# A decoder layer with retrieved experts: the pace of the gathers, a later exponential, wider selection matrices and rows loaded by chunk

## The chip, the cores and the metric

The kernel runs on 1 core of one Trainium2 chip. The metric is the device time in microseconds (us) of one execution. The core has five engines that each run their own instruction list in order: TensorE (PE in the profile; its weight loads are PEld), VectorE (DVE), ScalarE (ACT), GpSimd (POOL) and SyncE (SP), which here only starts DMA transfers. Engines wait for each other by semaphores.

## The reference

One layer works on 256 tokens of 2048 floats. It has an attention part with 16 heads, a retrieval of single-neuron experts (PEER), and a gated embedding, each followed by a layer norm. The change lies in the last two:

```python
    q = (xt @ wq).reshape(t, PEER_HEADS, PEER_QDIM)
    ...
    top, sel = lax.top_k(cand, PEER_TOPK)
    eidx = jnp.take_along_axis(cidx, sel, axis=-1)
    gates = jax.nn.softmax(top, axis=-1)
    ...
        ub = u[eb]
        vbk = v[eb]
        act = jax.nn.gelu(jnp.einsum('thed,td->the', ub, xb).astype(jnp.float32))
        w = (gb * act).astype(xb.dtype)
        return jnp.einsum('the,thed->td', w, vbk)
    ...
        gate = jax.nn.sigmoid(jnp.einsum('bsd,de->bse', x, ple_gate[i]))
        emb = jnp.einsum('bsk,kd->bsd', p[i], ple_proj[i])
        x = layer_norm(alpha * x + gate * emb, ln_g[i, 2], ln_b[i, 2])
```

There are 8 heads with 16 chosen experts each, so 128 experts per token, out of 16384 rows in `u` and `v`.

## The kernel before

The tokens are treated in two ways. For the first 100 tokens (groups of 64, 32 and 4, `GROUPS`) the chosen rows of `peer_u` and `peer_v` are gathered from memory. For the other 156 tokens all 16384 experts are computed densely, and a matrix of gates, zero almost everywhere, picks the chosen ones.

**Dense u stage** (L971 and L982). 128 blocks `u_block`, one for each `ia`: a load `wf` of 1 MB on SP's queue (a ring of 5 tiles), 16 matmuls in one PSUM bank (L208, two records each in the trace), and ScalarE's gelu L950, which empties the bank into `A1` (first 64 blocks) or `A2`. Four banks go round. Beside each of the first 64 blocks one step of `topk_work` runs: top-16 searches on VectorE, the choice among candidates (products L691 on POOL), and `gates(t)`, the softmax of the gates: subtract L707 on VectorE, exponential L711 on ScalarE, sum and division L714 to L716. A `yield` ends a step, so the number of yields says how many blocks lie between two parts of it in program order. Beside the blocks 64 to 127 `gate_work` runs: for 5 tokens at a time, VectorE compares to make one-hot matrices (L897, L899), ScalarE scales them (L903, L904), TensorE multiplies them in pairs into `ps_G` (L911, L912), and VectorE multiplies the result into `A1` (L921).

**Dense v stage** (L1024 and L1034). 128 blocks for the first half of the outputs, then 128 for the second; a block is 8 matmuls (L1000), and two blocks share a load of 1 MB. The first 64 run with `gate_work` for `A2`. The last six blocks are held back (`STAG`) and come after `sparse_out`.

**Gathers.** 200 transfers of 1 MB, 100 of u rows and then 100 of v rows, from `sparse_work`: each is a tiny DMA `mark` on SP's queue (L856), a copy of it on POOL (L857), and the indirect DMA on POOL (L859) into a ring of 4 tiles `gb`. SP's queue holds the marks between the loads, so a mark lands about when the loads ahead of it do, and POOL goes no further before. VectorE uses the gathered tile in L832 (product with the token, summed) or in L842 (weighted sum). `gathers(n)` adds `n` to `due` after every block and starts a gather whenever `due` reaches 1: `GQ` beside the queries, `GU` in the u stage, `GV` in the v stage. `sparse_out` (L869) then sums and transposes the weighted rows with selection matrices `sel`, 64, 32 and 4 columns wide, by matmuls L876.

**Gated embedding.** After layer norm 2 the transposed input `X2` is multiplied with `ple_gate` in four chunks of 512 columns (`gate_mm`), whose weights are split into a high and a low part by ScalarE (L109) and VectorE (L110). `gate_out` loads the embedding `em` on POOL's queue (L1128), takes the sigmoid on ScalarE (L1130), and multiplies and adds on VectorE (L1131, L1132). The `x2` that it adds to must be scaled by rows of layer norm 2 first: `natural_x2` loads `g_row` and `b_row`, copied to all partitions, and POOL does a multiplication and an addition (L578, L579) for each chunk and token half: chunk 0 with rows on POOL's queue, chunks 1 to 3 at once after chunk 0, with rows on SP's queue. `finish` normalizes and stores.

In code wrapped in `keep` an engine's instructions stay in the order in which the program lists them; the rest is placed by a scheduler.

Of the kernel before, what the change touches and what calls it, by code (L numbers as in the profile page):

```python
# [9 lines left out]
F32 = mybir.dt.float32  # L10
# [4 lines left out]
ALU = mybir.AluOpType  # L15
# [4 lines left out]
P = 128  # L20
T = 256
NT = T // P
D = 2048
ND = D // P
NCH = D // 512
# [13 lines left out]
SEG1 = 64  # L39
# [7 lines left out]
SELB = 8  # L47
NGB = 4

GQ = 1.8  # L50
GU = 0.7
GV = 0.35
GSCALE = 2.0 ** 15
GB = 5
OHB = 5
# [102 lines left out]
def build(tc, a, out):  # L158
    nc = tc.nc
# [367 lines left out]
    for c in range(NCH):  # L527
        s = slice(c * 512, (c + 1) * 512)
# [47 lines left out]
    def affine(xt, c, gr, br):  # L576
        s = slice(c * 512, (c + 1) * 512)
        nc.gpsimd.tensor_tensor(xt[:, s], xt[:, s], gr[:, s], op=ALU.mult)  # L578
        nc.gpsimd.tensor_tensor(xt[:, s], xt[:, s], br[:, s], op=ALU.add)  # L579
# [14 lines left out]
    gin = pools.open("gin", "left", bufs=1)  # L594
# [7 lines left out]
    nc.gpsimd.memset(zero, 0.0)  # L602
    sel, eig, eact, ew = [], [], [], []
    for i, (_, n) in enumerate(GROUPS):
        sel.append(gin.tile([P, n], F32, name=f"sel{i}"))
        nc.gpsimd.dma_start(sel[i], a[f"c_sel{i}"])

        eig.append(gin.tile([P, 2, n], U32, name=f"eig{i}"))
        eact.append(gin.tile([P, n], F32, name=f"eact{i}"))
        ew.append(gin.tile([P, n], F32, name=f"ew{i}"))  # L610
# [50 lines left out]
    keep = tc.keep_in_program_order  # L661
# [42 lines left out]
    def gates(t):  # L704

        g = gate[:, t]
        keep(nc.vector.tensor_tensor(g, CV[:, t], CV[:, t, :, 0:1].to_broadcast([P, PH, TOPK]),  # L707
                                     op=ALU.subtract))
        yield
        yield  # L710
        keep(nc.scalar.activation(g, g, AF.Exp))  # L711
        for _ in range(6):
            yield
        keep(nc.vector.tensor_reduce(gs[:, t], g, axis=AX.X, op=ALU.add))  # L714
        nc.vector.reciprocal(gs[:, t], gs[:, t])
        nc.vector.tensor_tensor(g, g, gs[:, t, :, None].to_broadcast([P, PH, TOPK]), op=ALU.mult)  # L716
        if t == 0:
            nc.vector.tensor_copy(eg[:NSP, 1].bitcast(F32), g[:NSP])
            for i in range(len(GROUPS)):
                slots(i, 1, by_slot(i, 1))  # L720
            gated.append(t)
        yield
# [69 lines left out]
    def gathers(n):  # L792

        nonlocal due
        due += n
        while due >= 1:
            due -= 1
            run(sparse, 1)
# [70 lines left out]
    def sparse_out():  # L869

        for i, (t0, n) in enumerate(GROUPS):
            per = min(ND, 512 // n)
            for d0 in range(0, ND, per):
                ps = pbank(pp, "ps_y")
                for j in range(per):
                    keep(nc.tensor.matmul(ps[:, j * n:(j + 1) * n],  # L876
                                          ys[i][:, (d0 + j) * P:(d0 + j + 1) * P], sel[i],
                                          start=True, stop=True))
                nc.scalar.copy(yT[:, d0:d0 + per, t0:t0 + n],
                               ps[:, :per * n].rearrange("p (j t) -> p j t", j=per))  # L880

    def gate_work(oh, parts, s0, ns, group):

# [76 lines left out]
    for hh in range(2 * PH):  # L960
# [3 lines left out]
        if hh > 2:  # L964
            gathers(GQ)
    bg.flush()
# [4 lines left out]
    for ia in range(SEG1):  # L971
        u_block(ia, W_of(ia))
        run(work, 1)
        gathers(GU)
    while not run(work, 1):
# [6 lines left out]
    for ia in range(SEG1, NIA):  # L982
        u_block(ia, W_of(ia))
        run(work, 1 + (ia % 8 == 7))
        gathers(GU)
    while not run(work, 1):
        pass

# [35 lines left out]
    for ia in range(NIA):  # L1024
        if ia >= SEG1:
            while not done:
                done = run(work, 1)
        v_block(0, ia, psv)
        if not done:
            done = run(work, 1 + (ia % 8 == 7))  # L1030
        gathers(GV)
    pools.close("ohp")
    psv2 = v_banks(pa)
    for ia in range(SEG1):  # L1034
        v_block(1, ia, psv2)
        gathers(GV)
    pools.close("a1p")
# [3 lines left out]
    x2 = [l2.tile([P, D], F32, name=f"x2_{t}") for t in range(NT)]  # L1041
# [29 lines left out]
    for ia in range(SEG1, NIA - STAG):  # L1071
        v_block(1, ia, psv2, keep if ia >= NIA - STAG - 16 else lambda ins: ins)
        gathers(GV)
        if ia in (NIA - STAG - 9, NIA - STAG - 5):
# [28 lines left out]
    l3 = pools.open("l3", "left", bufs=1)  # L1103
# [21 lines left out]
    def gate_out(c, t, ps, c0, n):  # L1125
        s = slice(c * 512 + c0, c * 512 + c0 + n)
        em = l3.tile([P, 512], F32, name="em", tag="em", bufs=3)[:, :n]
        keep(nc.gpsimd.dma_start(em, a["s_emb"][t * P:(t + 1) * P, s]))  # L1128
        sig = l3.tile([P, 512], F32, name="sig", tag="sig", bufs=3)[:, :n]
        keep(nc.scalar.activation(sig, ps, AF.Sigmoid))  # L1130
        keep(nc.vector.tensor_tensor(sig, sig, em, op=ALU.mult))  # L1131
        keep(nc.vector.scalar_tensor_tensor(x2[t][:, s], x2[t][:, s], ALPHA, sig,  # L1132
                                            op0=ALU.mult, op1=ALU.add))
        for j in range(c0, c0 + n, 256):
            nc.vector.bn_stats(st3[t][:, 2 * c + j // 256, :],
                               x2[t][:, c * 512 + j:c * 512 + j + 256])
# [18 lines left out]
    ln2(0)  # L1155
    ln2(1, range(ND // 8))

    g_row = l3.tile([P, D], F32, name="g_row", tag="g_row")
    b_row = l3.tile([P, D], F32, name="b_row", tag="b_row")

    def natural_x2(c0, c1, queue):

        s = slice(c0 * 512, c1 * 512)
        for dst, src in ((g_row, "ln_g"), (b_row, "ln_b")):
            keep(queue.dma_start(dst[:, s], a[src][1:2, s].to_broadcast([P, s.stop - s.start])))
        for c in range(c0, c1):
            for t in range(NT):
                affine(x2[t], c, g_row, b_row)


    sg.order = sg2.order = keep
# [3 lines left out]
    for half in range(2):  # L1175
        for t in range(NT):
            gate_mm(pss[t], t, parts[half], 0, 512, half * ND // 2)
        if not half:
            natural_x2(0, 1, nc.gpsimd)
    for c in range(NCH):  # L1180
        if c == NCH - 1:
            gate_out(c, 1, ps_half, 256, 256)
            break
        gate_out(c, 0, pss[0], 0, 512)
        first = gate_parts(c + 1, 0)
        gate_out(c, 1, pss[1], 0, 512)
        parts = first + gate_parts(c + 1, 1)
        if c == 0:
            natural_x2(1, NCH, nc.sync)
        if c == 1:  # L1190
            gr3, br3 = ln_rows(l3, 2)
        if c < NCH - 2:
            pss = [pbank(pa, "ps_gate") for _ in range(NT)]
            for t in range(NT):
                gate_mm(pss[t], t, parts, 0, 512)
            continue
        pss = [pbank(pa, "ps_gate") for _ in range(3)]
        gate_mm(pss[0], 0, parts, 0, 512)
        gate_mm(pss[1][:, :256], 1, parts, 0, 256)
        gate_mm(pss[2][:, :256], 1, parts, 256, 256)  # L1200
        gate_out(c + 1, 0, pss[0], 0, 512)
        gate_out(c + 1, 1, pss[1][:, :256], 0, 256)
        ps_half = pss[2][:, :256]
# [5 lines left out]
def _constants():  # L1209
    pos = np.arange(T, dtype=np.float32)  # L1210
    inv = np.float32(ROPE_THETA) ** (-np.arange(0, ROT, 2, dtype=np.float32) / np.float32(ROT))
    ang = (pos[:, None] * inv[None, :].astype(np.float32)).astype(np.float32)
    cos, sin = np.cos(ang).T, np.sin(ang).T
    h = ROT // 2
    C = np.ones((P, T), np.float32)
    S = np.zeros((P, T), np.float32)
    for s in (0, 64):
        C[s:s + h] = cos
        C[s + h:s + 2 * h] = cos
        S[s:s + h] = -sin  # L1220
# [6 lines left out]
    return {  # L1227
        "c_ropeC": C, "c_ropeS": S, 
        "c_svalid": svalid, "c_sneg": sneg,
        "c_dmask": np.concatenate([np.zeros((P, P), np.float32), dm], axis=1),  # L1230
        "c_tri": (r[:, None] >= r[None, :]).astype(np.float32),
        "c_ones": np.ones((P, P), np.float32),
        "c_ident": np.eye(P, dtype=np.float32),
        **{f"c_sel{i}": (np.arange(P)[:, None] // (P // n) == np.arange(n)[None, :]).astype(np.float32)
           for i, (_, n) in enumerate(GROUPS)},
        "c_iota": np.broadcast_to(np.arange(P, dtype=np.float32), (P, P)).copy(),
    }
# [71 lines left out]
```

## Time and profile before

| what | value |
|---|---|
| time, median of 3 runs | 1824.08 us (1823.42 to 1825.66) |
| the profiled execution | 1825.47 us |
| its span, first to last instruction | 1823.7 us |
| mean granted clock of TensorE | 0.988 |
| TensorE, matmuls | 1772.4 us busy |
| VectorE | 1058.7 us busy |
| ScalarE | 540.0 us busy |
| GpSimd | 548.6 us busy |
| DMA, the whole span | 609.04 MB, mean 334 GB/s |

Lines such as L950 are lines of the kernel. A window of the trace gives, for each engine, the busy time in that stretch with the number of instructions, then TensorE's granted clock (1.00 is full speed), the busy share of the DMA engines, and GB/s. In a wait, `PE ps_u L208 <- DMA wf<-peer_u` reads: TensorE at L208 waited for the transfer into `wf`. A timeline joins instructions of one kind into a row with its count; the bracket says how long the engine was idle before and what released it. A matmul of the u blocks, the v blocks and `sparse_out` leaves two records, and a row's count is that of records. A wait for several semaphores is put down to the one that came last.

### The profile page before, as it was taken

The page shows a single profiled execution, that of the slowest core. Times are in us where ns is not written, and L with a number is a line of the kernel's source. Part 1 is how long each engine was busy: PE and PEld are TensorE (multiplying, and loading weights), DVE is VectorE, ACT ScalarE, POOL GpSimd, SP SyncE. Part 2 cuts the span into 40 slices and gives each one's busy share as a digit, 9 for nine tenths or more (in the row PEclk, how much of TensorE's full clock was granted, in tenths as well). Part 3 has the DMA queues.
Part 4 walks back from the last instruction along what each step waited for, and adds up shares of the span by engine and source line. Part 5 has one row for each costly group of instructions (what it writes and reads, how often), then busy time and mean ns, then how long its engine had stood idle before and what let it go on. Part 6 is the DMA issues. An engine that isn't in the chain of part 4 may idle for free.

```text
span 1823.7 us, 30383 instructions
## 1 busy us (share of the span) xinstructions
PE 1772.4 (97%) x12110; PEld 1663.8 (91%) x12110; DVE 1058.7 (58%) x1659; ACT 540.0 (30%) x1351; POOL 548.6 (30%) x581
## 2 busy tenths in 40 slices
PE   8999999999998999999999999999999999999986
PEld 7888888888897999899999999999999999999866
DVE  5555688654588995545555546674343333333786
ACT  5687477642011001004333315550000000001532
POOL 0133133005465244232223222333243222221241
PEclk9999999999999999999999999999999999998999
DMA  7544644657899999999999999999999999997461
GB/s 281 189 167 162 231 147 155 234 204 263 310 376 415 415 420 419 421 420 420 411 401 406 399 404 407 371 379 387 420 420 420 419 418 417 421 420 330 155 256 52
DMA packets 99726, 609.04 MB, mean 334 GB/s; under 512 B 12872, under 2 KB 14720, under 8 KB 35424
## 3 DMA queue, kind: packets, MB, share of 16 engines
q1 hardware_dynamic: 66784, 384.24, 53.5%
q0 software_dynamic: 31072, 218.28, 29.7%
q10 hardware_dynamic: 1728, 4.59, 0.6%
q8 instruction: 95, 1.56, 0.3%
q14 instruction: 47, 0.39, 0.1%
HBM read 600.40 MB, written 6.55 MB: 333 GB/s over the span
## 4 chain that ended last, share of the span: by engine, by line
PE 85%; DMA 9%; DVE 4%; ACT 1%; issue 1%; POOL 0%; SPq 0%; DVEq 0%; ACTq 0%; POOLq 0%
PE ps_v L1000 27%; PE ps_u L208 25%; PE ps_qk L197 7%; PE ps_q L208 6%; DMA wf<-peer_u 4%; DMA wf<-peer_v 4%; PE ps_qk L199 3%; PE ps_v L216 2%; PE ps_v L217 2%; PE ps_mix L215 2%; PE ps_mix L216 2%; PE ps_mix L217 2%; PE ps_v L215 2%; DVE wl L110 1%; DMA gb<-u_rows,eig 1%; PE ps_gate L216 1%
## 5 line engine op out<-in xcount | busy, mean ns | idle before, releaser
L208 PE MATMUL ps_u<-XF,wf 128*128 128x156 f32 x4096 | 559.0, 298 | 15.5 <-ACT A L950 9.3
L208 PEld LDWEIGHTS ps_u<-XF,wf 128*128 128x128 f32 x4096 | 549.0, 191 | 18.4 <-ACT A L950 15.4
L1000 PE MATMUL ps_v<-A,wf 128*128 128x156 f32 x4096 | 555.7, 298 | 4.8 <-DMA wf<-peer_v 4.7
L1000 PEld LDWEIGHTS ps_v<-A,wf 128*128 128x128 f32 x4096 | 547.7, 191 | 7.3 <-DMA wf<-peer_v 6.7
L842 DVE SCALAR_TENSOR_TENSOR y<-gb,ew,y 128x2048 f32<-128x2048 f32 x94 | 221.0, 2351 | 258.0 <-DMA gb<-v_rows,eig 257.9
L832 DVE SCALAR_TENSOR_TENSOR gb<-gb,xq 128x2048 f32<-128x2048 f32 x100 | 229.1, 2295 | 171.5 <-DMA gb<-u_rows,eig 165.8
L110 DVE TENSOR_TENSOR wl<-wf,wh 128x1024 fp32r<-128x1024 f32 (+1 forms) x201 | 222.6, 1132 | 114.9 <-ACT wh L109 113.2
L109 ACT CAST wh<-wf 128x1024 fp32r<-128x1024 f32 (+1 forms) x201 | 173.1, 890 | 359.7 <-DMA wf<-ple_gate 250.3
L857 POOL COPY pace<-mark 1x1 f32<-1x1 f32 x200 | 107.2, 536 | 564.5 <-DMA mark<-c_iota 564.1
L197 PE MATMUL ps_qk<-X,wh 128*128 128x512 f32 x512 | 185.2, 401 | 0.0
L859 POOL DMA_INDIRECT gb<-u_rows,eig x100 | 126.7, 1267 | 145.2 <-DVE gb L832 62.2
L950 ACT ACTIVATE A<-ps_u 128x156 f32<-128x156 f32 x128 | 38.2, 301 | 433.3 <-PE ps_u L208 360.7
L859 POOL DMA_INDIRECT gb<-v_rows,eig x100 | 130.9, 1309 | 54.7 <-issue 32.2
L199 PE MATMUL ps_qk<-X,wl 128*128 128x256 f32 x512 | 145.7, 285 | 0.0
L197 PEld LDWEIGHTS ps_qk<-X,wh 128*128 128x128 f32 x512 | 96.4, 188 | 22.0 <-issue 1.0
L903 ACT ACTIVATE hi<-eq,ghf 128x64 f16<-128x64 f16 x312 | 104.5, 335 | 39.4 <-DVE eq L897 38.1
L208 PE MATMUL ps_q<-XF,wf 128*128 128x256 f32 x512 | 113.5, 379 | 0.0
L208 PEld LDWEIGHTS ps_q<-XF,wf 128*128 128x128 f32 x512 | 95.9, 190 | 12.3
L904 ACT ACTIVATE lo<-eq,glf 128x64 f16<-128x64 f16 x312 | 104.3, 334 | 0.0
L199 PEld LDWEIGHTS ps_qk<-X,wl 128*128 128x128 f32 x512 | 96.3, 188 | 2.5 <-issue 1.3
L1019 ACT COPY XF<-ps_v 128x312 f32<-128x312 f32 x8 | 3.4, 420 | 188.8 <-PE ps_v L1000 188.5
L216 PE MATMUL ps_gate<-wl,X 128*128 128x512 f32 (+1 forms) x144 | 53.9, 376 | 4.8 <-DVE wl L110 4.6
(242 smaller groups left out, 1768.0 us busy)
## 6 DMA issues: line engine op xcount, KB each, us to landing
wf<-peer_u SPq DMA_DIRECT2D x128, 1024.0 KB
wf<-peer_v SPq DMA_DIRECT2D x128, 1024.0 KB
wf<-w_qk SPq DMA_DIRECT2D x64, 512.0 KB
wf<-w_out SPq DMA_DIRECT2D x32, 512.0 KB
wf<-peer_wq SPq DMA_DIRECT2D x16, 1024.0 KB
wf<-ple_gate SPq DMA_DIRECT2D x16, 1024.0 KB
wf<-w_v SPq DMA_DIRECT2D x31, 512.0 KB
mark<-c_iota SPq DMA_DIRECT2D x200, 0.0 KB
```

The lines of the kernel that those rows point to most:

```text
L109: self.order(nc.scalar.copy(wh, src))
L110: self.order(nc.vector.tensor_tensor(wl, src, wh.bitcast(F32), op=ALU.subtract))
L197: nc.tensor.matmul(ps, wh[:, j * P:(j + 1) * P], xt[:, dt, :], start=dt == 0, stop=False)
L199: nc.tensor.matmul(ps[:, :T], wl[:, j * P:(j + 1) * P], xt[:, dt, :T], start=False, stop=dt == ND - 1)
L208: nc.tensor.matmul(ps[:, :T - t0], wf[:, dt * P:(dt + 1) * P], xt[:, dt, t0:], start=dt == 0, stop=dt == ND - 1)
L216: nc.tensor.matmul(ps, hi, wl, start=False, stop=False)
L832: keep(nc.vector.scalar_tensor_tensor(g, g, 1.0, xq[i], op0=ALU.mult, op1=ALU.mult, accum_out=eact[i][:, j:j + 1]))
L842: keep(nc.vector.scalar_tensor_tensor(ys[i], g, ew[i][:, j:j + 1], ys[i], op0=ALU.mult, op1=ALU.add))
L857: keep(nc.gpsimd.tensor_copy(pace, mark))
L859: keep(nc.gpsimd.indirect_dma_start(out=g, out_offset=None, in_=a[kind], in_offset=bass.IndirectOffsetOnAxis(ap=eig[i][:, 0, j:j + 1], axi ...
L903: nc.scalar.mul(hi[:, j, :], eq[:, j, :], ghf[:, t])
L1000: return nc.tensor.matmul(ps[:, (j % 2) * NDT:(j % 2 + 1) * NDT], vf[:, j * P:(j + 1) * P], W_of(ia), start=False, stop=ia == NIA - 1 and ...
```

## The change

Four edits, independent of each other.

- **Pacing of the gathers.** Blocks with one-hot products get a larger rate than those without: in the u stage 0.64 and 0.75 in place of 0.7, in the v stage 0.42 for the first 64 blocks and 0.33 for the rest in place of 0.35. The number of gathers stays.
- **Exponential of the gates.** Between the subtraction and the exponential lie nine yields in place of two.
- **Selection matrices.** They are at least 32 columns wide, so that of the third group grows from 4 to 32 (the added columns are zero), and its products are packed 16 to a bank; the copy takes the first `n` columns of each.
- **Rows for scaling.** `natural_x2` takes one chunk at a time, with its rows in a tile of two times 512 columns (two such tiles in turn). For chunks 1 to 3 it is called after the chunk before, with the rows on SP's queue; third-norm rows now get tiles of their own. The sigmoid's tile goes from three buffers to two.

```diff
-GU = 0.7
-GV = 0.35
+GU, GUG = 0.64, 0.75
+GV, GVG = 0.33, 0.42
...
-        sel.append(gin.tile([P, n], F32, name=f"sel{i}"))
+        sel.append(gin.tile([P, max(n, 32)], F32, name=f"sel{i}"))
...
                                      op=ALU.subtract))
-        yield
-        yield
+        for _ in range(9):
+            yield
         keep(nc.scalar.activation(g, g, AF.Exp))
...
         for i, (t0, n) in enumerate(GROUPS):
-            per = min(ND, 512 // n)
+            m = max(n, 32)
+            per = min(ND, 512 // m)
             for d0 in range(0, ND, per):
                 ps = pbank(pp, "ps_y")
                 for j in range(per):
-                    keep(nc.tensor.matmul(ps[:, j * n:(j + 1) * n],
+                    keep(nc.tensor.matmul(ps[:, j * m:(j + 1) * m],
                                           ys[i][:, (d0 + j) * P:(d0 + j + 1) * P], sel[i],
                                           start=True, stop=True))
                 nc.scalar.copy(yT[:, d0:d0 + per, t0:t0 + n],
-                               ps[:, :per * n].rearrange("p (j t) -> p j t", j=per))
+                               ps[:, :per * m].rearrange("p (j t) -> p j t", j=per)[:, :, :n])
...
     for ia in range(SEG1, NIA):
         u_block(ia, W_of(ia))
         run(work, 1 + (ia % 8 == 7))
-        gathers(GU)
+        gathers(GUG)
...
-        gathers(GV)
+        gathers(GVG if ia < SEG1 else GV)
...
-        sig = l3.tile([P, 512], F32, name="sig", tag="sig", bufs=3)[:, :n]
+        sig = l3.tile([P, 512], F32, name="sig", tag="sig", bufs=2)[:, :n]
...
-    def natural_x2(c0, c1, queue):
-
-        s = slice(c0 * 512, c1 * 512)
-        for dst, src in ((g_row, "ln_g"), (b_row, "ln_b")):
-            keep(queue.dma_start(dst[:, s], a[src][1:2, s].to_broadcast([P, s.stop - s.start])))
-        for c in range(c0, c1):
-            for t in range(NT):
-                affine(x2[t], c, g_row, b_row)
+    def natural_x2(c, queue):
+
+        s = slice(c * 512, (c + 1) * 512)
+        gb = l3.tile([P, 2, 512], F32, name="gb_rows", tag="gb_rows", bufs=2)
+        for i, src in enumerate(("ln_g", "ln_b")):
+            keep(queue.dma_start(gb[:, i], a[src][1:2, s].to_broadcast([P, 512])))
+        for t in range(NT):
+            nc.gpsimd.tensor_tensor(x2[t][:, s], x2[t][:, s], gb[:, 0], op=ALU.mult)
+            nc.gpsimd.tensor_tensor(x2[t][:, s], x2[t][:, s], gb[:, 1], op=ALU.add)
...
         parts = first + gate_parts(c + 1, 1)
-        if c == 0:
-            natural_x2(1, NCH, nc.sync)
+        natural_x2(c + 1, nc.sync)
         if c == 1:
             gr3, br3 = ln_rows(l3, 2)
```

The third group's products stay in one PSUM bank (16 x 32 = 512 columns).

More of the change, by code (lines that the diff above doesn't have):

```diff
@@ L1156, in build @@
     ln2(1, range(ND // 8))
-    g_row = l3.tile([P, D], F32, name="g_row", tag="g_row")
-    b_row = l3.tile([P, D], F32, name="b_row", tag="b_row")
-    def natural_x2(c0, c1, queue):
-        s = slice(c0 * 512, c1 * 512)
-        for dst, src in ((g_row, "ln_g"), (b_row, "ln_b")):
-            keep(queue.dma_start(dst[:, s], a[src][1:2, s].to_broadcast([P, s.stop - s.start])))
-        for c in range(c0, c1):
-            for t in range(NT):
-                affine(x2[t], c, g_row, b_row)
+    def natural_x2(c, queue):
[6 more added lines that the diff above has]
+            nc.gpsimd.tensor_tensor(x2[t][:, s], x2[t][:, s], gb[:, 1], op=ALU.add)
     sg.order = sg2.order = keep
@@ L1178, in build @@
         if not half:
-            natural_x2(0, 1, nc.gpsimd)
+            natural_x2(0, nc.gpsimd)
     for c in range(NCH):
@@ L1233, in _constants @@
         "c_ident": np.eye(P, dtype=np.float32),
-        **{f"c_sel{i}": (np.arange(P)[:, None] // (P // n) == np.arange(n)[None, :]).astype(np.float32)
+        **{f"c_sel{i}": (np.arange(P)[:, None] // (P // n) == np.arange(max(n, 32))[None, :]).astype(np.float32)
            for i, (_, n) in enumerate(GROUPS)},
```

## The prediction

> **What bounds the kernel now.** I read the page's head and its DMA part first, then the waits of TensorE, then windows cut at the edges of the stages, and last the timelines of the places where TensorE stands still.
>
> ```profile
> span 1823.7 us, 30383 instructions
> ...
> PE 1772.4 (97%) x12110; PEld 1663.8 (91%) x12110; DVE 1058.7 (58%) x1659; ACT 540.0 (30%) x1351; POOL 548.6 (30%) x581
> ...
> GB/s 281 189 167 162 231 147 155 234 204 263 310 376 415 415 420 419 421 420 420 411 401 406 399 404 407 371 379 387 420 420 420 419 418 417 421 420 330 155 256 52
> ...
> wf<-peer_u SPq DMA_DIRECT2D x128, 1024.0 KB
> wf<-peer_v SPq DMA_DIRECT2D x128, 1024.0 KB
> ```
>
> TensorE is busy for 97%, so an edit can win only the remaining 51 us and what runs at half clock. The GB/s line shows a second limit: from slice 12 to slice 35 (547 to 1641 us) it lies between 371 and 421 and never above. The transfers there are the expert weights, 1 MB each, and the 200 gathers, also 1 MB each (128 x 2048 floats, by the L842 row quoted below).
>
> ```profile
> PE ps_u L208 <- ACT A L950: 9.3, 2, 8.9
> PE ps_u L208 <- DMA wf<-peer_u: 6.2, 10, 1.9
> ...
> PE ps_v L1000 <- DMA wf<-peer_v: 4.7, 5, 2.2
> PE ps_gate L216 <- DVE wl L110: 4.6, 5, 1.7
> ...
> PE ps_G L911 <- ACT hi L903: 0.6, 1, 0.6
> ```
>
> Waits of TensorE: total, times, longest. One stall is on ScalarE's copy of a u block; ten waits are for u weights, five for v weights, five for the splits of the gate weights, and one of 0.6 us for a one-hot product.
>
> ```profile
> 540.00:660.00 120.00, 111.08 (x818) 110.73 (x817) 109.33 (x314) 10.27 (x30) 47.72 (x62) 0.96 1.01 416
> 660.00:719.00 59.00, 57.96 (x436) 57.55 (x436) 40.33 (x67) 7.29 (x19) 32.70 (x38) 1.00 1.01 419
> 719.00:785.00 66.00, 60.91 (x449) 59.24 (x447) 32.80 (x35) 5.19 (x18) 16.03 (x21) 1.00 1.01 421
> 838.00:1117.00 279.00, 279.00 (x2318) 277.64 (x2317) 149.09 (x179) 89.16 (x364) 79.92 (x90) 1.00 1.00 407
> 1117.00:1255.00 138.00, 138.00 (x1256) 135.97 (x1256) 91.24 (x111) 73.42 (x302) 37.69 (x40) 1.00 0.97 379
> 1255.00:1551.00 296.00, 296.00 (x2236) 296.00 (x2235) 115.50 (x50) 1.68 (x4) 94.34 (x96) 1.00 1.01 417
> 1551.00:1671.00 120.00, 115.15 (x843) 113.21 (x841) 48.01 (x28) 4.36 (x8) 31.18 (x36) 0.99 1.01 421
> ```
>
> Windows: length, busy time of PE, PEld, DVE, ACT, POOL, granted clock, DMA share, GB/s. The first three lie in the first 64 u blocks, the fourth in the other 64 (with one-hot products), the fifth in the v blocks with products, the last two in the v blocks after them. Where TensorE loses time, the DMA stands at 416 to 421; where it loses none, there is room (407 and 379). So the bytes of the stages without products are too many and those of the stages with products too few: 421 is my ceiling.
>
> **Edit 1, pacing.** A u block takes 4.24 us where nothing is late (timelines: start, length, engine, line, operation, and in brackets the idle time before and what ended it):
>
> ```profile
> 730.98 0.30 ACT L950 ACTIVATE A<-ps_u 128x156 f32<-128x156 f32 x1 [3.94 <-PE ps_u L208]
> 735.22 0.30 ACT L950 ACTIVATE A<-ps_u 128x156 f32<-128x156 f32 x1 [3.94 <-PE ps_u L208]
> ...
> 758.36 0.30 ACT L950 ACTIVATE A<-ps_u 128x156 f32<-128x156 f32 x1 [4.67 <-PE ps_u L208]
> 763.34 0.30 ACT L950 ACTIVATE A<-ps_u 128x156 f32<-128x156 f32 x1 [4.67 <-PE ps_u L208]
> ...
> 711.88 0.96 POOL L859 DMA_INDIRECT gb<-u_rows,eig  x1 [3.83 <-DVE gb L832]
> ...
> 716.85 0.96 POOL L859 DMA_INDIRECT gb<-u_rows,eig  x1 [3.83 <-DVE gb L832]
> ...
> 754.35 1.98 POOL L857 COPY pace<-mark 1x1 f32<-1x1 f32 x1 [5.04 <-DMA mark<-c_iota]
> ```
>
> At 758 a block takes 4.98 us, and it is a load that is late. Earlier, at 712, one gather is issued every 4.97 us and waits for its buffer, not for its pacing mark; the first long wait for a mark is at 754. So until about 750 the gathers are behind their program and take half of the DMA, whatever the pace says; a smaller pace only brings the end of this catching up nearer.
>
> Demand of a first-half u block: 1 load and 0.70 gathers of 1.0486 MB in 4.24 us is 420 GB/s, right at the ceiling, so a lost ring is never refilled. At 0.64 it is 406.
>
> Gain: from 534.59 (the first u block) to 754, less the 11.6 us of edit 2, lie about 46 blocks (208 us at some 4.5 each). While both kinds share evenly, a block works off 1 - 0.70 = 0.30 of a backlog, so about 14 gathers were behind; at 0.36 a block that takes 39 blocks. Seven blocks fewer at 0.74 us lost each are 5.2 us, and after them nothing pushes the demand to the ceiling. The bound from above: windows two and three hold 885 block matmuls of 4.24/32 us, 117.3 us of work in 125, so 7.7 us can be won; by bytes, 64 x 0.06 = 3.8 gathers fewer are 9.6 us of DMA at 421. I take 5.5; ends 2 and 7.7.
>
> Last v stage: a load feeds two v blocks (1.06 us for 8 matmuls each, 16 records), so 0.5 of a load and 0.35 gathers per block; at the 417 to 421 measured, 0.33 asks for 0.83/0.85 of it, 407 to 411. The wait is at the end: 843 matmuls of 0.1325 us are 111.7 us of work in 120, 8.3 lost, of which 4.7 is the listed wait. With 0.07 x 64 = 4.5 gathers more done before and 0.02 x 122 = 2.4 fewer issued here, the stage has some 4 MB (9 us of DMA) less to move. Two loads of gate weights (L1076) fall into it still, so not all goes. I take 5.5; ends 2 and 8.3.
>
> Given back: in the second half of u the demand rises to 407 x 1.75/1.70 = 419, under 421 by nothing much; in the v stage with products to 379 x 0.92/0.85 = 410. I take +1 for a few new waits; ends 0 and +10 (64 x 0.05 = 3.2 gathers plus 1 of backlog at 2.5 us).
>
> **Edit 2, the exponential of the gates 7 u blocks later.**
>
> ```profile
> 588.69 0.31 ACT L711 ACTIVATE gate<-gate 128x128 f32<-128x128 f32 x1 [22.17 <-DVE gate L707]
> ...
> 534.59 3.34 PE L208 MATMUL ps_u<-XF,wf 128*128 128x156 f32 x24
> ...
> 590.76 70.83 PE L208 MATMUL ps_u<-XF,wf 128*128 128x156 f32 x512 [8.92 <-ACT A L950]
> 662.08 4.48 PE L208 MATMUL ps_u<-XF,wf 128*128 128x156 f32 x32 [0.49 <-DMA wf<-peer_u]
> 667.11 13.09 PE L208 MATMUL ps_u<-XF,wf 128*128 128x156 f32 x97 [0.55 <-DMA wf<-peer_u]
> ```
>
> ScalarE runs in order: at L711 it stands 22.17 us for VectorE's subtract, which is deep in the top-k work. The block copies L950 queued behind it come late, the four PSUM banks fill, and TensorE stands 8.92 us; then it starts slowly (the window's mean clock is 0.96). Nine yields instead of two put seven blocks' copies, 7 x 4.24 = 30 us, ahead of L711, and 30 is more than 22: the stall goes. The first window prices it: 818 matmuls of 0.1325 us are 108.4 us of work in 120, so 11.6 were lost, 8.92 of it the gap. But 72 us later TensorE waits for a load anyway, and the DMA carried 416 of 421 all through: while TensorE stood, the loads filled the ring. What really comes free is 120 x (421 - 416)/421 = 1.4 us. I take 1; ends 0 and 11.6. The nine yields of the second token half lengthen the top-k work from 46 to 53 steps, one a block, still short of the 64 blocks after which the products need its results. The POOL products of L691 that stood in one clump come apart between gathers, which holds no buffer longer.
>
> **Edit 3, 32 columns for the last group.**
>
> ```profile
> 1670.61 7.23 PE L876 MATMUL ps_y<-sel,y 128*128 128x64 f32 x64
> 1677.67 6.61 PE L876 MATMUL ps_y<-sel,gb 128*128 128x4 f32 x32
> ...
> 1678.20:1688.20 10.00, 10.00 (x45) 9.97 (x46) 0.00 (x0) 0.47 (x2) 0.00 (x0) 0.50 0.01 4
> ```
>
> The 64- and 32-column matmuls start every 0.113 us, the 4-column ones every 0.207, with the clock at 0.50 from 1678.2 on, which costs 5 us in 10. The clock fell although TensorE had no gap; it fell when 64 narrow matmuls had been through, and 32 columns are narrow too. I take -0.5; ends 0 and -5. By the Trainium skill (TensorE: Matmul & The Clock Gate, Part 1: The HAM clock gate) half clock follows a window of some 3.4 us without activity; here no row shows such a gap, so by that rule alone the thin stream must have counted as idle, and 32 columns might count as busy, which would give the 5.
>
> **Edit 4, rows of the scaling chunk by chunk.**
>
> ```profile
> 1736.00:1765.00 29.00, 24.24 (x97) 17.27 (x96) 26.72 (x31) 9.32 (x18) 17.09 (x13) 1.00 0.61 222
> 1765.00:1787.00 22.00, 22.00 (x98) 18.08 (x97) 12.03 (x22) 9.51 (x19) 1.09 (x2) 1.00 0.52 204
> ...
> 1731.00 9.79 POOL L578 TENSOR_TENSOR x<-x,g_row 128x512 f32<-128x512 f32 x6 [12.60 <-DMA g_row<-ln_g]
> 1740.76 10.18 POOL L579 TENSOR_TENSOR x<-x,b_row 128x512 f32<-128x512 f32 x6
> ...
> 1735.26 12.84 DVE L110 TENSOR_TENSOR wl<-wf,wh 128x512 fp32r<-128x512 f32 x8
> ...
> 1752.19 4.89 DVE L110 TENSOR_TENSOR wl<-wf,wh 128x512 fp32r<-128x512 f32 x8
> ...
> 1752.91 0.50 PE L216 MATMUL ps_gate<-wl,X 128*128 128x512 f32 x1 [1.71 <-DVE wl L110]
> ```
>
> The gate matmuls of chunk 1 take 29 us, those of chunk 2, with as many, 22. POOL's twelve operations on chunks 1 to 3 (20 us in a row) lie beside them, and VectorE's eight splits take 12.84 us beside POOL and 4.89 without: VectorE is busy 26.72 of 29. Now POOL does four (6.7 us) after each chunk's rows, two 256 KB rows instead of two of 768 KB, so they also land sooner than 1731 and lie beside the products of sigmoid before the eight splits. The fours for chunks 2 and 3 fall where VectorE has 10 us to spare in 22. The rows' DMAs now stand on SP between gate loads, each 0.3 us of issue; the em transfers on POOL stand behind four operations at a time, no longer behind twelve. One wait of the 1.71 kind stays. I take -5; ends 0 and -7. Two sigmoid tiles instead of three make the third sigmoid wait for an add that ended long before; the last ones after the matmuls are ordered by VectorE's own work: 0, within 0.5 either way.
>
> **Sum.** -5.5 -5.5 +1 -1 -0.5 -5 = -16.5 us. The profiled execution took 1825.47 (span 1823.7 plus 1.8 around it), so 1809.0; it was 1.39 above the median of 1824.08, so the median to expect is 1807.6, say 1808.
>
> **Rivals.**
> *More is kept* (0.15). All three upper ends that the DMA allows: first half of u 9.6 + 1.4 = 11 instead of 6.5, last v stage 8.3 instead of 5.5, full clock at 1678 5 instead of 0.5. That is 11.8 more: 1796. For it: the byte count; against it: the catching up has to be paid first.
>
> *VectorE's time beside POOL moves, it does not go* (0.12). The twelve operations are as many as before; if the fours hit the splits just as the six did, each four costs VectorE 2.6 us again and TensorE waits in all three chunks: tail 0, time 1813. The Trainium skill (SBUF — State Buffer, Who interferes with whom) speaks for it: it has the two engines take turns on a shared port, one blocked for the other's whole instruction. The 12.84 against 4.89 agrees; only the slack in the other chunks speaks against it.
>
> *The pace gives nothing net* (0.12). The gathers taken out of the first stages meet 419 of 421 in the second half of u: waits of 10 us instead of 1, the v stage gains only 2. Then 1824.08 - 5.5 - 1 - 0.5 - 5 - 2 + 10 = 1820; half of this case counts as no change.
>
> *Late gathers hold the products* (0.08), the slower side.
>
> ```profile
> L842 DVE SCALAR_TENSOR_TENSOR y<-gb,ew,y 128x2048 f32<-128x2048 f32 x94 | 221.0, 2351 | 258.0 <-DMA gb<-v_rows,eig 257.9
> ```
>
> VectorE waits in order for gathers, 258 us in all, and the one-hot compares and the scaling of the gates stand behind that wait. In the v stage with products it is busy 91 of 138 us; 4.5 gathers more at 2.35 make it 102, 74%. If DMA at 410 to 419 makes each of the 48 + 27 gathers of the two product stages land 0.4 us later than the one-hot tiles made ahead can cover, TensorE waits 30 us, of which the loads that land meanwhile give back 10, as many as the third rival charges for them: 1808 + 30 - 10 = 1828. It decides once a gather's wait is longer than the lead of two groups, 9 us (31 groups of five tokens in 138 us); with the single wait of 0.6 us for products, the lead is ample now.
>
> **How the numbers follow.** The forecast has 0.53, with its own range 1801 to 1814 (the ends of the tail and of the two pacing terms, not all at once). With the rivals at 1796, 1813, 1820 and 1828 a range from 1793 to 1820 leaves out the slower case, part of the third, and a little of the first: about 0.2. Differences under 0.2% (3.6 us) can't be told from no change. Faster: 0.53 + 0.15 + 0.12 + half of 0.12 = 0.86; same 0.06; slower 0.08.
>
> **What would show it.** Pacing: in the first half of u waits for loads under 3 us instead of 6.2, and POOL waiting for marks before 730; in the last v stage no wait over 1 us; in the second half of u DMA at 415 or more and waits under 2 us. Exponential: ACT's wait at L711 under 5 us and no 8.92 gap, yet TensorE waiting for loads sooner than 120 us after the first u block. Narrow matmuls: still about 0.2 us each. Tail: chunk 1 in 22 to 25 us, eight splits in 5 to 7 us. I am wrong if TensorE waits for one-hot products, if the second half of u goes below 98% busy, or if the first half gains the stall's whole 11.6.

## The result and the profile after

The changed kernel takes 1799.59 us (median of 4 runs, 1796.47 to 1801.24), the kernel before 1824.54 beside it (1823.42 to 1825.66). The ratio is 0.9861 with a 95% interval of 0.9844 to 0.9878: 25 us less, where the forecast had 16.5 and 1808. The profiled execution took 1799.64 us. Line numbers of the changed kernel are one or two higher (L208 is L209, L711 is L712, L876 is L878, L950 is L952, L1000 is L1002, L1130 is L1132); in some of the experiments they are one lower than that.

The head of the page after, and the waits of TensorE after:

```profile
span 1797.9 us, 30384 instructions
...
PE 1764.4 (98%) x12110; PEld 1660.1 (92%) x12110; DVE 1059.9 (59%) x1659; ACT 540.7 (30%) x1351; POOL 568.7 (32%) x581
...
GB/s 280 190 165 163 234 150 149 209 208 283 301 346 418 416 416 416 420 421 421 420 420 420 420 417 420 410 420 401 421 421 418 404 412 413 421 421 398 94 286 89
```

```profile
PE ps_u L209 <- DMA wf<-peer_u: 8.8, 14, 1.1
...
PE ps_v L1002 <- DMA wf<-peer_v: 1.2, 2, 0.7
```

The wait on ScalarE's copy (8.9 us at one place) is gone, the wait for the gate weights' splits too. The wait for v weights fell from 4.7 to 1.2 us. The wait for u weights did not fall: 8.8 us in 14 pieces, before 6.2 in 10. Slices 20 to 24 of the GB/s line (counted from 0), 399 to 407 in the kernel before, are now at 417 to 420: the room beside the products is used up.

Windows of the changed kernel. The first four are cut where the copies of the u blocks 0, 16, 32, 48 and 64 start, then come the second half of u, the v blocks with products, two stretches of the last v stage, and the gate matmuls of chunks 1 and 2:

```profile
539.70:607.50 67.80, 67.80 (x512) 67.56 (x510) 57.49 (x172) 7.78 (x20) 31.22 (x38) 1.00 1.01 416
607.50:681.90 74.40, 69.56 (x514) 68.35 (x515) 59.81 (x167) 5.01 (x19) 17.96 (x24) 1.00 1.01 418
681.90:749.70 67.80, 67.80 (x514) 67.80 (x513) 46.48 (x59) 7.88 (x20) 39.00 (x44) 1.00 1.01 418
749.70:824.30 74.60, 70.78 (x535) 69.22 (x535) 38.45 (x44) 12.91 (x50) 16.60 (x23) 1.00 1.01 420
838.00:1105.00 267.00, 265.90 (x2193) 263.98 (x2193) 146.91 (x175) 83.34 (x339) 86.19 (x92) 1.00 1.01 420
1105.00:1256.00 151.00, 151.00 (x1351) 148.84 (x1351) 108.79 (x120) 76.74 (x312) 53.35 (x52) 1.00 1.00 411
1256.00:1551.00 295.00, 295.00 (x2229) 295.00 (x2228) 108.46 (x47) 1.67 (x4) 103.80 (x92) 1.00 1.01 415
1551.00:1652.00 101.00, 99.84 (x751) 99.37 (x751) 39.02 (x23) 4.36 (x8) 27.44 (x29) 1.00 1.01 420
1719.00:1741.00 22.00, 21.97 (x97) 17.70 (x96) 17.01 (x26) 9.50 (x18) 6.44 (x6) 1.00 0.89 300
1741.00:1763.00 22.00, 22.00 (x98) 18.04 (x97) 18.41 (x27) 9.49 (x18) 7.89 (x7) 1.00 0.63 227
```

The same marks in both profiles, and in three of the experiments below, say where the time went (start of ScalarE's copy, or of the matmul, in us; "end" is the end of the last busy instruction):

| mark | before | after | e1 rates | e2 exponential | e10 all but exponential |
|---|---|---|---|---|---|
| copy of u block 16 | 619.1 | 607.5 | 619.7 | 606.6 | 619.4 |
| copy of u block 64 | 837.8 | 824.3 | 827.3 | 837.0 | 824.6 |
| first v matmul | 1118.2 | 1106.6 | 1108.3 | 1117.3 | 1105.6 |
| first selection matmul | 1670.6 | 1652.3 | 1655.0 | 1669.5 | 1650.9 |
| first gate matmul | 1710.4 | 1693.7 | 1694.7 | 1709.3 | 1692.3 |
| last gate matmul ends | 1809.4 | 1785.8 | 1794.7 | 1808.4 | 1784.2 |
| end | 1820.0 | 1794.3 | 1805.2 | 1818.9 | 1792.7 |

From the second and third column: 13.5 us are won by block 64, 1.9 given back up to the first v matmul, 6.7 won up to the selection matmuls, 1.6 given back up to the gate matmuls, 6.9 won in them and 2.1 behind them.

### The profile page after: what moved, and what is told of

The parts are those of the page before. It is cut to its first block, busy times and chain, and to the rows that moved or that the text cites. A ratio compares the mean times of both kernels' runs of the same rounds, so it can differ in the third digit from the quotient of the medians.

```text
span 1797.9 us, 30384 instructions
## 1 busy us (share of the span) xinstructions
PE 1764.4 (98%) x12110; PEld 1660.1 (92%) x12110; DVE 1059.9 (59%) x1659; ACT 540.7 (30%) x1351; POOL 568.7 (32%) x581
## 4 chain that ended last, share of the span: by engine, by line
PE 91%; DMA 7%; DVE 1%; ACT 0%; issue 0%; SPq 0%; DVEq 0%; POOL 0%; ACTq 0%
PE ps_v L1002 30%; PE ps_u L209 26%; PE ps_qk L198 7%; PE ps_q L209 6%; DMA wf<-peer_u 5%; PE ps_qk L200 3%; PE ps_v L217 2%; PE ps_v L218 2%; PE ps_v L216 2%; PE ps_mix L216 2%; PE ps_mix L218 1%; PE ps_mix L217 1%; PE ps_gate L217 1%; PE ps_gate L218 1%; PE ps_gate L216 1%; PE ps_y L878 1%
## 5 line engine op out<-in xcount | busy, mean ns | idle before, releaser
L209 PE MATMUL ps_u<-XF,wf 128*128 128x156 f32 x4096 | 555.3, 297 | 9.5 <-DMA wf<-peer_u 8.8
L209 PEld LDWEIGHTS ps_u<-XF,wf 128*128 128x128 f32 x4096 | 544.8, 190 | 13.5 <-ACT A L952 7.3
L1002 PE MATMUL ps_v<-A,wf 128*128 128x156 f32 x4096 | 553.2, 297 | 1.2 <-DMA wf<-peer_v 1.2
L1002 PEld LDWEIGHTS ps_v<-A,wf 128*128 128x128 f32 x4096 | 546.3, 191 | 2.1 <-DMA wf<-peer_v 1.6
L858 POOL COPY pace<-mark 1x1 f32<-1x1 f32 x200 | 127.4, 637 | 517.0 <-DMA mark<-c_iota 516.5
L952 ACT ACTIVATE A<-ps_u 128x156 f32<-128x156 f32 x128 | 38.4, 300 | 445.8 <-PE ps_u L209 368.5
L860 POOL DMA_INDIRECT gb<-v_rows,eig x100 | 143.9, 1439 | 57.7 <-issue 23.2
L860 POOL DMA_INDIRECT gb<-u_rows,eig x100 | 115.4, 1154 | 144.8 <-DVE gb L833 54.9
L209 PE MATMUL ps_q<-XF,wf 128*128 128x256 f32 x512 | 113.6, 379 | 0.0
L209 PEld LDWEIGHTS ps_q<-XF,wf 128*128 128x128 f32 x512 | 95.9, 190 | 12.6 <-ACT eb L553 0.3
L216 PE MATMUL ps_v<-wh,X 128*128 128x512 f32 x128 | 49.7, 403 | 5.2 <-ACT wh L110 5.2
```

The costliest lines, as they stand in the source:

```text
L209: nc.tensor.matmul(ps[:, :T - t0], wf[:, dt * P:(dt + 1) * P], xt[:, dt, t0:], start=dt == 0, stop=dt == ND - 1)
L216: nc.tensor.matmul(ps, hi, wh, start=start, stop=False)
L858: keep(nc.gpsimd.tensor_copy(pace, mark))
L860: keep(nc.gpsimd.indirect_dma_start(out=g, out_offset=None, in_=a[kind], in_offset=bass.IndirectOffsetOnAxis(ap=eig[i][:, 0, j:j + 1], axi ...
L1002: return nc.tensor.matmul(ps[:, (j % 2) * NDT:(j % 2 + 1) * NDT], vf[:, j * P:(j + 1) * P], W_of(ia), start=False, stop=ia == NIA - 1 and ...
```

## The experiments

**The four edits one by one.** The first carries the four rates alone:

```diff
-GU = 0.7
-GV = 0.35
+GU, GUG = 0.64, 0.75
+GV, GVG = 0.33, 0.42
```

> Only edit 1 (the four rates). Theory A, transferred bytes decide when the first 64 u blocks end: 3.8 gathers fewer at 2.5 us each bring block 64 forward by 6 to 9.6 us, with the 8.92 us stall on the exponential still there, and the last v stage by 5 to 7; together 11 to 16 us less than before, about 1811. Theory B, the 13.5 us that the whole change won at block 64 were mostly the stall: the rates alone bring block 64 forward by 2 to 4 us, and the time is about 1816.

It took 1810.02 us (1809.22 to 1811.1; ratio 0.9913, 0.9897 to 0.993), 14.6 less than the kernel before. Block 64 came 10.5 us sooner, the stretch from there to the first v matmul was 0.6 longer, and the one up to the selection matmuls 5.7 shorter. Theory A holds. The first two rows are windows of the kernel before and of this one from block 48 to block 64, the third is this kernel's wait for u weights:

```profile
758.40:837.80 79.40, 73.60 (x526) 71.17 (x527) 35.10 (x37) 12.11 (x48) 25.92 (x27) 0.98 1.01 421
```

```profile
756.70:827.30 70.60, 69.21 (x529) 68.72 (x530) 30.45 (x35) 12.03 (x48) 21.78 (x23) 1.00 1.01 420
```

```profile
PE ps_u L208 <- DMA wf<-peer_u: 1.6, 4, 0.5
```

The last sixteen blocks went from 79.4 to 70.6 us: 8.8 of the 10.5. The stretch up to block 48 gained only 1.7: up to 726 us, where POOL's copy of a mark first waits long for it, the gathers left over from the query stage are behind their marks, and the rate has little hold on them.

The second carries the nine yields alone:

```diff
-        yield
-        yield
+        for _ in range(9):
+            yield
```

> Only edit 2 (nine yields ahead of the exponential). Theory A, bytes decide: the 8.92 us gap is gone and block 16 is some 11 us earlier, but by block 64 at most 1.4 us are left, because the gathers that were due take the DMA's time later; time 1822 to 1824. Theory B, the stall is kept: block 64 is 6 to 11 us earlier, since late gathers may be made up for beside the blocks with products, where the DMA has room (407 of 421 GB/s); time 1814 to 1818.

It took 1824.99 us (ratio 0.9999, 0.9988 to 1.0009): nothing. At block 16 it is 12.5 us ahead of the kernel before, at block 64 only 0.8. Its wait for u weights, and the window in which the gain is lost:

```profile
PE ps_u L208 <- DMA wf<-peer_u: 12.5, 23, 1.1
```

```profile
606.60:756.30 149.70, 139.91 (x1024) 135.96 (x1022) 110.52 (x239) 12.74 (x38) 61.43 (x75) 1.00 1.01 419
```

The 8.9 us at one place came back as 6.3 us more of small waits (12.5 against 6.2) and the slower start behind each, with the DMA at 419. Theory A again.

The third carries `natural_x2` by chunk and the two sigmoid tiles (the second half of the diff above).

> Only edit 4 (rows chunk by chunk, two sigmoid tiles). The gate matmuls of chunk 1 go from 29.2 us to 22 to 23, and nothing before them changes. If the 2.1 us that the whole change won after the last matmul belong to this edit, the time is 9 us less, 1815 to 1816; if they come from somewhere else, 7 us less, about 1817.5. If VectorE's time beside GpSimd only moved, chunks 2 and 3 would be 2 to 3 us longer each and the gain under 3 us.

It took 1815.96 us (ratio 0.9944, 0.9927 to 0.9961), 8.7 less. Chunk 1 took 22.0 us in place of 29.2, chunk 2 as before; its window:

```profile
1736.00:1757.00 21.00, 21.00 (x93) 17.24 (x92) 16.39 (x26) 9.43 (x18) 5.26 (x6) 1.00 0.82 295
```

The 2.1 us behind the last gate matmul are in this run too (8.5 us to the end, before 10.6), so they belong to this edit.

The fourth carries the 32 columns (`max(n, 32)`).

> Only edit 3 (32 columns for the last group). If thin columns are what halves the clock there, the 32 matmuls take 3.6 us instead of 6.6 and the time falls by 3 to 5 us. If the number of columns up to 32 doesn't matter, they take 6.3 to 7 us as before and the time is unchanged within 1 us.

It took 1823.78 us (ratio 0.9992, 0.9982 to 1.0001): unchanged. Its last 32 selection records took as long as before, at half clock:

```profile
1674.78 7.01 PE L877 MATMUL ps_y<-sel,gb 128*128 128x32 f32 x32
...
1675.00:1681.00 6.00, 6.00 (x30) 6.00 (x30) 0.00 (x0) 0.59 (x1) 0.00 (x0) 0.50 0.09 37
```

The four alone give 14.6 - 0.3 + 8.7 + 0.9 = 23.9 us, the whole change 25: nothing is left for an interplay of any size.

**The exponential at the new rates.** The changed kernel with two yields again:

```diff
-        for _ in range(9):
-            yield
+        yield
+        yield
```

> The changed kernel with two yields ahead of the exponential, as before the change. By the run of the rates alone, whose block 64 came 10.6 us sooner against 13.5 with both edits, the exponential is worth 3 us at these rates: 1802 to 1804, although it was worth nothing by itself. If the two edits don't depend on each other, it is worth the same 0 to 1 us as alone: 1800.

It took 1798.12 us (1795.55 to 1799.81; ratio 0.9858, 0.9843 to 0.9873), less than either case and no more than the changed kernel; the 3 us that I had read from two profiles were not there. Its timeline has the gap in full, and then 651 records without a pause:

```profile
591.79 88.39 PE L208 MATMUL ps_u<-XF,wf 128*128 128x156 f32 x651 [9.53 <-ACT A L951]
```

It is 11.9 us behind the changed kernel at block 16 and 0.3 behind at block 64. Without the stall, in the changed kernel, TensorE waits for loads from 612 us on:

```profile
612.52 4.48 PE L209 MATMUL ps_u<-XF,wf 128*128 128x156 f32 x32 [0.48 <-DMA wf<-peer_u]
```

With it the same time is lost in one piece, and TensorE's waits for u weights come to 0.2 us in all. Gathers issued up to block 64's copy in the kernel before, the changed one and this one:

```profile
L859 POOL DMA_INDIRECT gb<-u_rows,eig x70 | 87.5, 1250 | 130.8 <-DVE gb L832 61.3 <-DVE TV L637 24.2 <-DMA wf<-peer_wq 22.5
```

```profile
L860 POOL DMA_INDIRECT gb<-u_rows,eig x65 | 73.4, 1129 | 130.1 <-DVE gb L833 53.2 <-DVE TV L638 35.8 <-DMA wf<-peer_wq 22.7
```

```profile
L859 POOL DMA_INDIRECT gb<-u_rows,eig x65 | 81.8, 1259 | 102.6 <-DVE gb L832 34.4 <-DMA wf<-peer_wq 22.3 <-DVE TV L637 21.4
```

70 against 65 and 65: five gathers at 2.5 us are 12.5 us of DMA, and block 64 came 13.5 and 13.2 us sooner. The other profiles fit. The exponential alone has 70 gathers and block 64 at 837.0, the rates alone 66 and 827.3, so the 3 us between the rates alone and the changed kernel are one gather. The runs below with lower rates have 64, 62, 62 and 58 gathers, and block 64 at 820.2, 818.1, 817.4 and 815.9. From 70 to 62 that is 2.5 us for each gather. The last four won only 2.2 us: there TensorE's own pace comes near, 4.24 us a block, by which 64 blocks from the first copy at 539.5 us end at 811. The number of gathers tells when block 64 is done; the stall does not.

**Still fewer gathers in the first stage.** First:

```diff
-GU, GUG = 0.64, 0.75
-GV, GVG = 0.33, 0.42
+GU, GUG = 0.58, 0.75
+GV, GVG = 0.34, 0.45
```

> The changed kernel with rates 0.58 / 0.75 / 0.45 / 0.34 (first u half, second u half, v with products, v after) in place of 0.64 / 0.75 / 0.42 / 0.33. If the transferred bytes set the end of the first 64 blocks, 3.8 gathers fewer bring block 64 forward by 6 to 9 us against the changed kernel, the later stages give back up to 3, and the time is 1791 to 1796. If it is the gathers left over from the query stage, which run at their own pace until 778 us whatever the rate, only the last ten blocks gain: 2 to 3 us, about 1797.

It took 1794.49 us (ratio 0.9837, 0.9818 to 0.9856). Block 64 came 6.2 us before that of the changed kernel, and the v blocks after the products (from block 64 of the v stage to the first selection matmul) gave back 3.8, with 399.8 us in place of 396.0. The interval touches that of the changed kernel (0.9844 to 0.9878), so the gain of 5 us rests on these marks as much as on the times. Waits for weights:

```profile
PE ps_v L1002 <- DMA wf<-peer_v: 4.3, 3, 2.1
...
PE ps_u L209 <- DMA wf<-peer_u: 2.3, 5, 1.1
```

Then further in the same direction, `GU, GUG = 0.52, 0.77` and `GV, GVG = 0.35, 0.46`:

> As the run before, with 0.52 / 0.77 / 0.46 / 0.35. The first u half would be bound by TensorE alone (at most 1.5 us of waits for loads), but the second u half asks for 407 x 1.77/1.70 = 424 GB/s and the last v stage for 421: both at or over the ceiling of 421. Bytes theory: what the first half wins beyond the run before comes back as waits in the second half and at the end of the v stage; time within 3 us of the run before. If the ceiling is not hard, it is 3 us or more faster than that.

It took 1801.36 us (ratio 0.9871, 0.9853 to 0.9889). Block 64 came 8.4 us before that of the changed kernel and the first v matmul 9.5, but the first selection matmul 3.3 us behind it; the last v stage waits most:

```profile
PE ps_v L1002 <- DMA wf<-peer_v: 9.0, 11, 2.6
```

The sign is as the bytes say, but the loss is 7 us against the run before where I had expected at most 3. None of it lies in the second half of u, although 424 was asked there: from block 64 to the first v matmul it took 281.2 us, the run before 281.1. Nearly all of it lies in the v blocks after the products, 408.2 us against 399.8. A rate of 0.35 there is that of the kernel before, with its demand of 420.

**Wider selection matrices.** The changed kernel with 128 columns in all three groups:

```diff
-        sel.append(gin.tile([P, max(n, 32)], F32, name=f"sel{i}"))
+        sel.append(gin.tile([P, max(n, 128)], F32, name=f"sel{i}"))
...
-            m = max(n, 32)
+            m = max(n, 128)
```

> The changed kernel with all three selection matrices 128 columns wide. If narrow matmuls halve the clock, the 96 records start every 0.11 us to the end, the clock stays at 1.00 until the wait before the transposes of layer norm 2, and the time is 4 to 5 us less, 1794 to 1796. If the number of columns has nothing to do with it, the clock falls to 0.50 some 7 us after their start as before, and the time is unchanged or up to 2 us more.

It took 1792.63 us (ratio 0.9824, 0.9806 to 0.9842). Selection matmuls of the changed kernel with two windows (its 32-column records begin at 1655.8), and the same of this one with one window:

```profile
1652.29 7.88 PE L878 MATMUL ps_y<-sel,y 128*128 128x64 f32 x64
1659.99 7.01 PE L878 MATMUL ps_y<-sel,gb 128*128 128x32 f32 x32
...
1656.00:1660.00 4.00, 4.00 (x33) 4.00 (x32) 0.00 (x0) 0.59 (x1) 0.00 (x0) 0.83 0.99 410
1660.00:1664.00 4.00, 4.00 (x20) 4.00 (x21) 0.00 (x0) 0.58 (x1) 0.00 (x0) 0.50 0.18 76
```

```profile
1651.69 7.31 PE L877 MATMUL ps_y<-sel,y 128*128 128x128 f32 x64
1658.84 3.74 PE L877 MATMUL ps_y<-sel,gb 128*128 128x128 f32 x32
...
1658.00:1664.00 6.00, 6.00 (x53) 6.00 (x53) 0.00 (x0) 1.22 (x6) 0.00 (x0) 1.00 0.21 87
```

The clock stays at 1.00, the last 32 records take 3.74 us in place of 7.01, and the transposes of layer norm 2 begin 20.6 us after their end in place of 23.4. The gain is larger than either case said: from the first selection matmul to the transposes it is 6.6 us. Four times the columns cost nothing, since 64 records still take 7.3 us. Then 64 columns:

> The changed kernel with selection matrices of 64 columns in the second and third group. If the clock follows the columns that stream through, half of 128 isn't enough: it falls to 0.50 within 10 us of the start and the time is 1797 to 1800. If 64 are enough, the last 32 records take 3.6 us and the time is that of 128 columns, 1792 to 1794.

It took 1794.25 us (ratio 0.9836, 0.9821 to 0.9851), and this is its last group, with a window from its middle group on:

```profile
1660.66 3.74 PE L877 MATMUL ps_y<-sel,gb 128*128 128x64 f32 x32
...
1658.00:1664.00 6.00, 6.00 (x56) 6.00 (x56) 0.00 (x0) 0.93 (x3) 0.00 (x0) 1.00 0.46 191
```

64 columns are enough, 32 were not. Nothing between was run.

**Both together.** Rates of 0.58 / 0.75 / 0.45 / 0.34 and 128 columns:

> The changed kernel with the rates 0.58 / 0.75 / 0.45 / 0.34 and selection matrices of 128 columns together. The one gains in the first u half, the other after the last v load, so they should add: 5 us and 7 us below the changed kernel, about 1787.5. If they meet in the last v stage, where the rates leave more waits for loads and the clock starts lower, 1790 to 1792.

It took 1790.4 us (1788.39 to 1792.45; ratio 0.9813, 0.98 to 0.9827). The two gains, 5.1 and 7.0 us by the runs of each, add up to all but 3 us. In its profile the v blocks after the products took 403.6 us, at the same rates as in the run of the rates (399.8), so these 3 us may be scatter; the last v stage waits as in that run:

```profile
PE ps_v L1001 <- DMA wf<-peer_v: 4.6, 3, 3.1
```

And with a little less taken from the first stage and the low rate kept in the last:

```diff
-GU, GUG = 0.58, 0.75
-GV, GVG = 0.34, 0.45
+GU, GUG = 0.60, 0.75
+GV, GVG = 0.33, 0.45
```

> Matrices of 128 columns and rates of 0.60 / 0.75 / 0.45 / 0.33: the last v stage keeps the low rate of the changed kernel, and the first u half gets most of the relief. By bytes block 64 comes some 2 us later than with 0.58 and the last v stage loses about 4 us less: 1787 to 1789. If the waits at the end of the v stage come from the loads of the gate weights there, not from the rate, they stay and the time is 1791 to 1793.

It took 1789.7 us (1788.28 to 1792.6; ratio 0.9811, 0.9797 to 0.9825), between the two cases and not to be told from the run before. Its wait for v weights fell from 4.6 to 0.6 us, which speaks for the rate and against the loads of the gate weights: in the six profiles with a rate of 0.33 there this wait is 0.6 to 3.4 us, with 0.34 it is 4.3 and 4.6. TensorE's wait for u weights rose from 2.8 to 4.7 us, and a pause of 1.9 us stands between its selection matmuls, for which the profile shows no cause. The v blocks after the products took 395.5 to 398.4 us in those six, 399.8 and 403.6 at 0.34, and 400.9 to 408.2 at 0.35 (five). It is 10 us faster than the changed kernel and 35 faster than the kernel before.

## Why the prediction was right, and where its terms were off

**Rates, first half of u: the term that was mis-sized.** The prediction took 5.5, the rates alone won 10.5. The failing step is "Seven blocks fewer at 0.74 us lost each are 5.2 us, and after them nothing pushes the demand to the ceiling": it priced the sooner end of the catching up and put nothing on the second half of the same sentence. The gain lies where it had no term, in blocks 48 to 64, where the kernel before lost 9.7 us (526 records of 0.1325 us are 69.7 of work in 79.4) because a demand of 420 leaves an emptied ring empty (inferred from these windows and from the 70.6 us at 0.64; no view shows the ring itself). The upper bound of 7.7 ended with the window at 785 us, in the middle of that loss; the other bound, 9.6 by bytes, was within 1 us of what came. One of the signs of being wrong came true in its number: with both edits the first half won 13.5, more than the stall's whole 11.6. The single runs clear the stall of it, with 10.5 by the rates and 0.8 by the exponential. The sign of waits for loads under 3 us held in the run of the rates alone (1.6), not in the changed kernel (8.8).

**Exponential.** The prediction took 1 of the stall's 11.6 us, by the DMA's 416 of 421 GB/s. Alone it took 0.3 us more, at the new rates it made no difference that can be seen. The change does what it says (ScalarE gets to the exponential without a wait), and it is worth nothing:

```profile
590.89 1.28 ACT L712 ACT_TABLE_LOAD   x1
592.18 0.31 ACT L712 ACTIVATE gate<-gate 128x128 f32<-128x128 f32 x1
```

The sign that was named for it, waits for loads sooner after the first block, came at 612 us in place of 662. The forecast that POOL would wait for marks before 730 holds in the run of the rates alone (first row), not in the changed kernel (second): with the stall gone the blocks come sooner and the gathers stay behind for longer.

```profile
726.13 0.18 POOL L857 COPY pace<-mark 1x1 f32<-1x1 f32 x1 [4.36 <-DMA mark<-c_iota]
```

```profile
764.88 0.18 POOL L858 COPY pace<-mark 1x1 f32<-1x1 f32 x1 [4.33 <-DMA mark<-c_iota]
```

**Last v stage and what was given back.** 5.5 forecast; the window 1551 to 1652 has 751 records, 99.5 us of work in 101, so 1.5 us are lost where 8.3 were: 6.8 won. Given back: +1 forecast, 1.9 measured between block 64 and the first v matmul, with the DMA at 420 of 421. The forecast of 419 and 410 GB/s by the ratio of the rates came out as 420 and 411. That of 407 to 411 for the last v stage did not: its two windows show 415 and 420. TensorE showed no longer wait for one-hot products, so the slower rival had no place; nor had the one in which the rates give nothing.

**Narrow matmuls.** Forecast -0.5 because 32 columns would be narrow too: the run of this edit alone agrees (0.9992, within no change), and the clock was 0.50 as before. The price of 5 us that the rival put on it was real, as the runs with 64 and 128 columns show; the change just did not pad far enough. The prediction had the clock fall after "64 narrow matmuls"; that row counts records, so they are 32 matmuls, half of them 64 columns wide, and in the changed kernel the clock fell within the 32-column ones. By the Trainium skill (TensorE: Matmul & The Clock Gate, Part 1: The HAM clock gate) the clock halves after a window without activity. The runs here agree only if a stream of 32 columns counts as too little activity, for TensorE had no gap: the same 96 records keep the full clock at 64 columns and lose it at 32.

**Rows by chunk.** Forecast -5 with an end of -7, measured -6.9 in the chunk. The splits beside POOL in chunks 1, 2 and 3 of the changed kernel:

```profile
1718.51 5.21 DVE L111 TENSOR_TENSOR wl<-wf,wh 128x512 fp32r<-128x512 f32 x8
...
1738.52 7.42 DVE L111 TENSOR_TENSOR wl<-wf,wh 128x512 fp32r<-128x512 f32 x8
...
1758.44 8.52 DVE L111 TENSOR_TENSOR wl<-wf,wh 128x512 fp32r<-128x512 f32 x8
```

Over the undisturbed 4.89 they lose 0.3, 2.5 and 3.6 us, together 6.5, where before one lot lost 8.0. So the rival was right in its mechanism, that VectorE's time beside POOL moves and does not go, and the rule of the Trainium skill (SBUF — State Buffer, Who interferes with whom) that one of the two is blocked while the other works through their shared port agrees with it; but VectorE is busy 17 to 18.4 of 22 us in chunks 1 and 2, and TensorE doesn't notice.

The tail's other 2.1 us were not foreseen ("the last ones after the matmuls ... 0, within 0.5 either way"). The third-last sigmoid of the kernel before and of the changed one:

```profile
1802.41 0.60 ACT L1130 ACTIVATE sig<-ps_gate 128x512 f32<-128x512 f32 x1 [10.68 <-PE ps_gate L217]
```

```profile
1776.20 0.60 ACT L1132 ACTIVATE sig<-ps_gate 128x512 f32<-128x512 f32 x1 [8.06 <-PE ps_gate L218]
```

It starts 7.0 us ahead of the last gate matmul's end before (1809.4), and 9.6 after (1785.8). The last chunk's matmuls are placed by the scheduler, which now finishes the first token half sooner, so VectorE is through with it when the second half comes. Which line of the edit made the scheduler do so was not tried.

Sum of the terms by the profile: -13.5 + 1.9 - 6.7 + 1.6 - 6.9 - 2.1 = -25.7, where the forecast had -6.5 + 1 - 5.5 - 0.5 - 5 + 0. The +1.6 between the selection and the gate matmuls was in no term and may be scatter: that stretch took 39.8 us before and 41.4 after, but also 41.4 in the run of the rows alone (1669.0 to 1710.4), which changes nothing there, and 39.8 again in the run with a rate of 0.52, whose last group has 32 columns too. The direction and the places of the three large gains were right; their sizes together were a third too small. The time lies outside the forecast's own range (1801 to 1814) and nearer to the faster rival, at 1796: by bytes that rival gave the first half of u 11 where 13.5 came, and the last v stage 8.3 where 6.7 came, but its 5 for the clock did not come at 32 columns.

## What to carry to other kernels

Where a stage stands at the DMA's ceiling, count the bytes that have to be moved by its end, and price an edit by the bytes that it takes out; a stall of another engine is worth nothing there, because the loads catch up while it lasts. A rate that asks for just the ceiling is worse than it looks: a ring emptied once stays empty to the end of the stage, so leave a few per cent of room (here a demand of 406 under a ceiling of 421), and move the rest to stages that have it, but to each only as much as it has. Pad narrow matmuls far enough that the granted clock stays up, and check it in the windows.

## What the hardware showed that was not expected

TensorE's clock fell to 0.50 in a stream of selection matmuls without any gap when their last groups were 32, or 32 and 4, columns wide, and stayed at 1.00 with 64 or 128. Until it fell, the records followed each other every 0.11 us in all of them. Against 128 columns it cost 6.6 us: 0.6 in the first 64 records (7.88 against 7.31), 3.3 in the last 32 (7.01 against 3.74) and 2.7 in the stretch behind them (23.4 against 20.6).
